# Keeping both halves of split projection weights in DRAM, instead of the low half alone

## The chip, the cores and the metric

One core of one Trainium2 chip runs the whole program. The metric is the device time of one execution in microseconds (us). A kernel's time is the median of its runs; beside it stands one execution that the profiler recorded, and all durations below come from that one. The engines are PE (TensorE, with PEld for its weight loads), DVE (VectorE), ACT (ScalarE), POOL (GpSimd) and SP (SyncE, which here only issues transfers).

## The reference, cut to what matters

The program is one decoder block on 1024 tokens of width 1024. What matters here are its three dense projections, which run for every token:

```
h    = rms_norm(x, norm1_g) * (1 + scale1) + shift1
proj = h @ w_in + b_in                  # 1024 x 2304: q, k, v and three conv inputs
mix  = concat([attn, conv]) @ w_out + b_out          # 1024 x 1024
x    = x + gate1 * mix
h2   = rms_norm(x, norm2_g) * (1 + scale2) + shift2
q    = h2 @ w_query                     # 1024 x 2048: 16 half-queries of 128
# top-16 of 128 keys per half-query, top-16 pairs, then 128 experts per token:
x    = x + gate2 * sum_k gate_k * gelu(h2 . peer_u[idx_k]) * peer_v[idx_k]
y    = rms_norm(x, final_g)
```

All arrays are float32.

## The kernel before

**Two parts.** The *front* computes everything up to the choice of experts, for three groups of token tiles one after the other: `GROUPS = [[0,1,2],[3,4,5],[6,7]]`, a tile being 128 tokens. They are called g0, g1 and g2. The *dense part* (from line 1073) then multiplies five tiles with all 16384 experts (A at line 1133, V at line 1179), while three tiles are done by gathering rows (lines 960 to 990). The dense part's order is written out by hand (`manual_schedule`, line 1323). In the front, the order on each engine is made by the scheduler from its own timeline; the program's order is only what it starts from.

**A projection block.** The weights lie in DRAM as 42 blocks of 1024 x 128 (18 of `w_in`, 8 of `w_out`, 16 of `w_query`), each 512 KB. A group passes through all 42, so 126 blocks are used in all. To keep float32 precision, a weight block is split into a high part H (rounded to the type fp32r) and a low part L = w - H; the activations are split likewise. `lin` (line 269) does three products for each of two halves q of the block, in this order: H x hH, H x hL, L x hH, four matmuls each, so 24 matmuls for a block. L is first used at the ninth matmul of a block (and at the ninth of its second half's twelve), H at the first.

**Where H and L come from.** `Weights.load` (line 215) runs one block ahead of `lin` in the program's order. In all three groups it loads the raw block (line 223, tag `wraw`, two buffers) and lets ACT cast each half to H (line 230, tag `wH`, four buffers, that is two blocks). In g0, POOL computes L (line 232), and one block later SP writes L to a DRAM tile `low` (line 225). In g1 and g2, L is read back from `low` (line 235) into its buffers (tag `wL`, four). A buffer of H or of L can be refilled when the matmuls of the block two before have read it; a raw buffer as soon as its block's two casts are done (in g0 also the two subtractions). All of these transfers are issued by SP, in order, together with the loads of x (line 352), of the adaptive-norm weights (`wada`, line 750, in g0 only), of the keys (line 631) and the stores of `x1` (line 610) and `h2` (line 623).

**What runs beside it.** In g0, DVE works through `wada` (lines 754 and 756) in the first 130 us. In g1 and g2, `dense_gates1` (line 817) builds the gate matrices of the dense tiles: DVE, POOL and ACT make one-hot rows `oh` (lines 834, 843, 847), PE multiplies them (G, line 857), ACT copies the result to `stg` (line 858) and stores it to DRAM (`G_d`, line 860, 2 MB a store, 20 stores, issued from ACT's queue). In the query stage of each group (16 blocks), ACT copies the projection out (line 640), PE multiplies it with the keys (`pk`, line 643), and DVE takes the top 16 (lines 141 to 145). ACT further evicts the output projection (`os`, line 585) and normalises rows (line 321).

Of the kernel before, what the change touches and what calls it, by code (L numbers as in the profile page):

```python
# [9 lines left out]
F32 = mybir.dt.float32  # L10
F32R = mybir.dt.float32r
# [7 lines left out]
P = 128  # L19
# [3 lines left out]
NC = D // P  # L23
# [61 lines left out]
def block_kernel(  # L85
# [18 lines left out]
    nc = tc.nc  # L104
    cst = ctx.enter_context(tc.tile_pool(name="cst", bufs=1))
    dr = ctx.enter_context(tc.tile_pool(name="dr", bufs=1, space=bass.MemoryType.DRAM))
# [46 lines left out]
    with ExitStack() as fctx:  # L153
        sl_ = slx.enter_context(tc.tile_pool(name="sl", bufs=1, side="right"))
        fs = fctx.enter_context(tc.tile_pool(name="fs", bufs=1))
# [46 lines left out]
        class Weights:  # L202


            def __init__(self):
                self.src = [(w_in, k) for k in range(18)] + [(w_out, k) for k in range(NC)]
                self.src += [(w_query, k) for k in range(16)]
                self.n = len(self.src)
                self.src *= len(GROUPS)
                self.at, self.ready = 0, []  # L210

                self.low = [dr.tile([P, 2, NC // 2, P], F32, name=f"low{k}") for k in range(self.n)]
                self.keep = []

            def load(self):
                if self.at == len(self.src):
                    return
                dram, k = self.src[self.at]
                name = f"{self.at}"
                low, first = self.low[self.at % self.n], self.at < self.n  # L220
                self.at += 1
                raw = fs.tile([P, NC, P], F32, tag="wraw", name=f"raw_{name}", bufs=2)
                nc.sync.dma_start(raw.rearrange("p c j -> p (c j)"), dram[k])
                while self.keep:
                    nc.sync.dma_start(*self.keep.pop(0))
                for q in range(2):
                    src = raw[:, q * (NC // 2) : (q + 1) * (NC // 2), :]
                    H = fs.tile([P, NC // 2, P], F32R, tag="wH", name=f"H_{name}_{q}", bufs=4)
                    L = fs.tile([P, NC // 2, P], F32R, tag="wL", name=f"L_{name}_{q}", bufs=4)
                    nc.scalar.copy(H, src)  # L230
                    if first:
                        nc.gpsimd.tensor_tensor(L, src, H.bitcast(F32), op=ALU.subtract)
                        self.keep.append((low[:, q], L.bitcast(F32)))
                    else:
                        nc.sync.dma_start(L.bitcast(F32), low[:, q])
                    self.ready.append((H, L))

            def take(self):
# [11 lines left out]
        class Front:  # L250
# [18 lines left out]
            def lin(self, name):  # L269
# [3 lines left out]
                for o, w, a, n in self.chunks:  # L273
                    ps = bank("a", f"lin_{self.key}{name}_{a}")
                    k = 0
                    for q, (H, L) in enumerate(parts):
                        for wt, h in ((H, self.hH), (H, self.hL), (L, self.hH)):
                            for c in range(NC // 2):
# [601 lines left out]
        def finish(i, acc):  # L880


            def load(name, src):
                t = row(f"{name}{i}")
                nc.sync.dma_start(t, src)
                return t

            g2 = load("g2", g2_d[0].partition_broadcast(P))
            yield
            yield  # L890
            yield
            nc.vector.tensor_tensor(acc, acc, g2, op=ALU.mult)
            xr = load("xr", x1_d[i])
            yield
            yield
            yield
            nc.vector.tensor_tensor(acc, acc, xr, op=ALU.add)
            fg = load("fg", final_g.partition_broadcast(P))
            yield
            ss = cst.tile([P, 1], F32, tag="ssf", name=f"ssf{i}", bufs=2)  # L900
            nc.scalar.activation(xr, acc, AF.Square, accum_out=ss)
            nc.scalar.activation(ss, ss, AF.Sqrt, scale=1.0 / D, bias=eps)
            yield
            yield
            r = cst.tile([P, 1], F32, tag="rf", name=f"rf{i}", bufs=2)
            nc.vector.reciprocal(r, ss)
            nc.vector.scalar_tensor_tensor(xr, acc, r, fg, op0=ALU.mult, op1=ALU.mult)
            yield
            nc.sync.dma_start(out[i * P : (i + 1) * P, :], xr)
# [163 lines left out]
    def dense_experts():  # L1073
# [19 lines left out]
        def split_U(b, part):  # L1093
            if part == 0:
                H = dp.tile([P, NC, P], F32R, tag="UH", name=f"UH{b}", bufs=2)
                nc.scalar.copy(H, Ur[b])  # L1096
# [312 lines left out]
```

## Time and profile before

| | us |
|---|---|
| median of three runs | 2824.21 |
| lowest and highest run | 2823.27, 2829.01 |
| the profiled execution, its own time | 2822.61 |
| its span, first to last instruction | 2820.8 |
| g0 in the trace | 0 to about 318 |
| g1 | about 318 to 667 |
| g2 | about 667 to 980 |
| dense part | about 980 to 2821 |

A stage is named by its group and its weights: g0-in, g1-o, g2-q and so on. The limits are read from the first and last matmuls of each group's blocks. The projections, with all that the change touches, end with g2; nothing in the dense part reads a projection weight.

### The profile page before, as it was taken

To read this page: it belongs to the slowest core of one execution; us is meant where nothing else is said; L and a number is where in the kernel's file an instruction comes from. 1 tells how busy PE (TensorE), PEld (TensorE's weight loads), DVE (VectorE), ACT (ScalarE), POOL (GpSimd) and SP (SyncE) were. 2 spreads that over 40 slices of the span, in tenths; PEclk is the share of its full clock that TensorE was granted. 3 is DMA by queue.
4 is the path that set the end of the run, shared out by engine and by line. 5 is a ranking of instruction groups with operands and counts; after the bars stand their busy time and mean duration, and the time that the engine had idled before them with its cause. 6 is when DMAs were issued, how large, how long until landed. Compare 5 with 4: busy or idle time off the path is not lost.

```text
span 2820.8 us, 44152 instructions
## 1 busy us (share of the span) xinstructions
PE 2642.3 (94%) x15358; PEld 2405.9 (85%) x15358; DVE 2165.8 (77%) x4645; ACT 1033.5 (37%) x2219; POOL 1696.2 (60%) x1726
## 2 busy tenths in 40 slices
PE   5998989988898869999999999999999999999997
PEld 4788977888788869999999899999998899999996
DVE  8835996879786877787777777777877777777776
ACT  3345555664667432222222222222222322222222
POOL 2334533523333247778777677777776777777771
PEclk9999999999999989999999999999999999999999
DMA  9757669986689949898889898989888888889884
GB/s 345 285 182 245 210 201 290 277 290 210 171 224 263 293 132 342 311 339 327 327 321 332 286 350 315 341 310 338 321 325 324 331 325 327 326 324 334 313 326 145
DMA packets 418268, 816.70 MB, mean 290 GB/s; under 512 B 192630, under 2 KB 198774, under 8 KB 418044
## 3 DMA queue, kind: packets, MB, share of 16 engines
q0 software_dynamic: 110592, 402.70, 38.8%
q1 hardware_dynamic: 143292, 369.24, 37.2%
q10 hardware_dynamic: 164160, 41.94, 6.9%
q8 instruction: 120, 1.97, 0.3%
q14 instruction: 104, 0.85, 0.1%
HBM read 739.83 MB, written 73.94 MB: 288 GB/s over the span
## 4 chain that ended last, share of the span: by engine, by line
PE 72%; DVE 13%; DMA 5%; issue 4%; ACT 3%; POOL 2%; SPq 0%; ACTq 0%; DVEq 0%; POOLq 0%
PE A L1133 29%; PE V L1179 29%; PE G L857 3%; PE lin_g1in L279 2%; DVE oh L834 2%; DVE adaacc L756 2%; DMA G_d<-stg 1%; PE lin_g0o L279 1%; DMA wada<-in_w_ada_dram 1%; PE lin_g2in L279 1%; PE po L430 1%; DVE Skg L143 1%; DVE ti L145 1%; PE lin_g2o L279 1%; DVE ti L142 1%
## 5 line engine op out<-in xcount | busy, mean ns | idle before, releaser
L960 POOL DMA_INDIRECT u<-in_peer_u_dram,idx x384 | 365.8, 952 | 264.5 <-DVE u L981 126.7
L1179 PE MATMUL V<-VH,WH 128*128 128x512 f32 x1280 | 501.4, 392 | 12.9 <-DVE acc_d L1186 10.3
L988 DVE SCALAR_TENSOR_TENSOR acc<-v,wv,acc 128x1024 f32<-128x1024 f32 x381 | 489.4, 1285 | 15.1 <-DMA v<-in_peer_v_dram,idx 10.9
L1179 PE MATMUL V<-VL,WH 128*128 128x512 f32 x1280 | 500.1, 391 | 0.0
L1179 PE MATMUL V<-VH,WL 128*128 128x512 f32 x1280 | 499.3, 390 | 0.0
L960 POOL DMA_INDIRECT v<-in_peer_v_dram,idx x384 | 363.5, 947 | 210.7 <-DVE u L981 69.1
L981 DVE SCALAR_TENSOR_TENSOR u<-u,h 128x1024 f32<-128x1024 f32 x384 | 457.7, 1214 | 5.8 <-DMA u<-in_peer_u_dram,idx 5.8
L1138 ACT ACTIVATE A<-A 128x384 f32<-128x384 f32 (+1 forms) x256 | 107.7, 422 | 955.7 <-PE A L1133 940.9
L1133 PE MATMUL A<-hDH,UH 128*128 128x384 f32 (+1 forms) x2048 | 345.5, 311 | 18.7 <-ACT UH L1096 18.1
L1116 POOL TENSOR_TENSOR VL<-V,VH 128x512 fp32r<-128x512 f32 x256 | 332.0, 1310 | 34.9 <-ACT VH L1112 32.6
L1133 PE MATMUL A<-hDH,UL 128*128 128x384 f32 (+1 forms) x2048 | 343.3, 310 | 8.5 <-POOL UL L1100 8.5
L1133 PEld LDWEIGHTS A<-hDH,UH 128*128 128x128 f32 x2048 | 321.9, 190 | 29.5 <-ACT UH L1096 18.9
L1133 PE MATMUL A<-hDL,UH 128*128 128x384 f32 (+1 forms) x2048 | 342.9, 310 | 0.0
L1100 POOL TENSOR_TENSOR UL<-U,UH 128x1024 fp32r<-128x1024 f32 x128 | 308.8, 2413 | 31.9 <-ACT UH L1096 29.7
L1133 PEld LDWEIGHTS A<-hDH,UL 128*128 128x128 f32 x2048 | 311.8, 189 | 9.8 <-POOL UL L1100 9.8
L1150 DVE TENSOR_TENSOR A<-A,Gb 128x384 f32<-128x384 f32 (+1 forms) x256 | 126.2, 498 | 248.3 <-ACT A L1138 243.6
L1133 PEld LDWEIGHTS A<-hDL,UH 128*128 128x128 f32 x2048 | 312.6, 190 | 0.0
L1179 PEld LDWEIGHTS V<-VH,WH 128*128 128x128 f32 x1280 | 241.3, 188 | 60.7 <-DVE acc_d L1186 12.0
L847 POOL TENSOR_TENSOR oh<-oh,gT 128x512 f32<-128x512 f32 x120 | 131.3, 1095 | 261.8 <-DVE oh L834 207.5
L1179 PEld LDWEIGHTS V<-VH,WL 128*128 128x128 f32 x1280 | 241.3, 188 | 51.4
L1179 PEld LDWEIGHTS V<-VL,WH 128*128 128x128 f32 x1280 | 241.3, 189 | 45.3
L1186 DVE TENSOR_TENSOR acc_d<-acc_d,V 128x512 f32<-128x512 f32 x310 | 211.7, 683 | 84.9 <-PE V L1179 84.8
(313 smaller groups left out, 4190.8 us busy)
## 6 DMA issues: line engine op xcount, KB each, us to landing
U<-in_peer_uT_dram SPq DMA_DIRECT2D x128, 512.0 KB, 7.7
V<-in_peer_v_dram SPq DMA_DIRECT2D x256, 256.0 KB, 3.8
L<-low SPq DMA_DIRECT2D x168, 256.0 KB, 4.0
G_d<-stg ACTq DMA_DIRECT2D x20, 2048.0 KB, 16.7
Gb<-G_d SPq DMA_DIRECT2D x64, 640.0 KB, 7.4
raw<-in_w_in_dram SPq DMA_DIRECT2D x54, 512.0 KB, 4.7
wada<-in_w_ada_dram SPq DMA_DIRECT2D x48, 512.0 KB, 6.8
raw<-in_w_query_dram SPq DMA_DIRECT2D x48, 512.0 KB, 5.2
```

The source lines that it names most:

```text
L279: nc.tensor.matmul(ps[:, :w], wt[:, c, :], h[:, q * (NC // 2) + c, o : o + w], start=(k == 0), stop=(k == 3 * NC - 1),)
L847: nc.gpsimd.tensor_tensor(og, og, gT[:, t0 : t0 + 4].unsqueeze(2).to_broadcast([P, 4, NK]), op=ALU.mult)
L960: nc.gpsimd.indirect_dma_start(out=t, out_offset=None, in_=peer_u if which == "u" else peer_v, in_offset=bass.IndirectOffsetOnAxis(ap=idx[ ...
L981: nc.vector.scalar_tensor_tensor(t, t, 1.0, h2[i], op0=ALU.mult, op1=ALU.mult, accum_out=av[i][:, j : j + 1])
L988: nc.vector.scalar_tensor_tensor(acc[i], t, wv[i][:, j : j + 1], acc[i], op0=ALU.mult, op1=ALU.add)
L1100: nc.gpsimd.tensor_tensor(L, Ur.pop(b), Up[b][0].bitcast(F32), op=ALU.subtract)
L1116: nc.gpsimd.tensor_tensor(L, Vr.pop(v), Vp[v][0].bitcast(F32), op=ALU.subtract)
L1133: nc.tensor.matmul(ps[:, : n * P], u[:, c, :], h[:, c, sl], start=(k == 0), stop=(k == 3 * NC - 1))
L1138: nc.scalar.activation(w, w, AF.Gelu)
L1150: nc.vector.tensor_tensor(w3, w3, g, op=ALU.mult)
L1179: nc.tensor.matmul(ps, w[:, ts_], v, start=(n == 0), stop=(n == 3 * CB - 1))
L1186: nc.vector.tensor_tensor(accs[0][:, t, hs], accs[0][:, t, hs], ps, op=ALU.add)
```

## The change

The first group writes both H and L of each half to DRAM, in one tile `HL`, and the second and third groups read that tile back. In those two groups there is no raw load and no cast any more.

```diff
-                self.low = [dr.tile([P, 2, NC // 2, P], F32, name=f"low{k}") for k in range(self.n)]
+                self.kept = [dr.tile([P, 2, 2, NC // 2, P], F32, name=f"kept{k}") for k in range(self.n)]
...
                 name = f"{self.at}"
-                low, first = self.low[self.at % self.n], self.at < self.n
+                kept, first = self.kept[self.at % self.n], self.at < self.n
                 self.at += 1
-                raw = fs.tile([P, NC, P], F32, tag="wraw", name=f"raw_{name}", bufs=2)
-                nc.sync.dma_start(raw.rearrange("p c j -> p (c j)"), dram[k])
+                if first:
+                    raw = fs.tile([P, NC, P], F32, tag="wraw", name=f"raw_{name}", bufs=2)
+                    nc.sync.dma_start(raw.rearrange("p c j -> p (c j)"), dram[k])
                 while self.keep:
                     nc.sync.dma_start(*self.keep.pop(0))
                 for q in range(2):
-                    src = raw[:, q * (NC // 2) : (q + 1) * (NC // 2), :]
-                    H = fs.tile([P, NC // 2, P], F32R, tag="wH", name=f"H_{name}_{q}", bufs=4)
-                    L = fs.tile([P, NC // 2, P], F32R, tag="wL", name=f"L_{name}_{q}", bufs=4)
-                    nc.scalar.copy(H, src)
+                    HL = fs.tile([P, 2, NC // 2, P], F32R, tag="wHL", name=f"HL_{name}_{q}", bufs=4)
+                    H, L = HL[:, 0], HL[:, 1]
                     if first:
+                        src = raw[:, q * (NC // 2) : (q + 1) * (NC // 2), :]
+                        nc.scalar.copy(H, src)
                         nc.gpsimd.tensor_tensor(L, src, H.bitcast(F32), op=ALU.subtract)
-                        self.keep.append((low[:, q], L.bitcast(F32)))
+                        self.keep.append((kept[:, q], HL.bitcast(F32)))
                     else:
-                        nc.sync.dma_start(L.bitcast(F32), low[:, q])
+                        nc.sync.dma_start(HL.bitcast(F32), kept[:, q])
                     self.ready.append((H, L))
```

A write in g0 grows from 256 to 512 KB (84 of them). In g1 and g2 a block is read by two transfers of 512 KB, where it was one of 512 KB (raw) and two of 256 KB (L); the bytes are the same. H and L of a half now share one buffer.

## Rows read from the trace of the kernel before

**Rows 1.** The profile's page: span, engines' busy time, lines of the chain that ended last.

```profile
span 2820.8 us, 44152 instructions
...
PE 2642.3 (94%) x15358; PEld 2405.9 (85%) x15358; DVE 2165.8 (77%) x4645; ACT 1033.5 (37%) x2219; POOL 1696.2 (60%) x1726
...
PE A L1133 29%; PE V L1179 29%; PE G L857 3%; PE lin_g1in L279 2%; DVE oh L834 2%; DVE adaacc L756 2%; DMA G_d<-stg 1%; PE lin_g0o L279 1%; DMA wada<-in_w_ada_dram 1%; PE lin_g2in L279 1%; PE po L430 1%; DVE Skg L143 1%; DVE ti L145 1%; PE lin_g2o L279 1%; DVE ti L142 1%
```

**Rows 2.** Busy time by stage; last columns: PE clock, DMA share, GB/s.

```profile
46.00:130.00 84.00, 81.13 (x435) 69.28 (x435) 76.23 (x140) 34.54 (x83) 31.84 (x22) 0.98 0.85 306
...
222.00:318.00 96.00, 86.69 (x515) 84.46 (x513) 73.19 (x453) 53.66 (x115) 57.07 (x123) 0.95 0.72 242
...
497.00:568.00 71.00, 65.69 (x448) 62.87 (x448) 57.75 (x76) 47.81 (x130) 37.76 (x37) 0.98 0.91 273
...
896.00:980.00 84.00, 74.06 (x578) 72.68 (x577) 69.09 (x347) 42.13 (x97) 24.61 (x76) 0.92 0.90 282
980.00:2820.00 1840.00, 1787.09 (x9997) 1630.03 (x9995) 1414.21 (x2153) 508.77 (x991) 1330.43 (x1129) 0.99 0.86 312
```

**Rows 3.** Groups of ACT in 318 to 980: count, busy us, mean ns, idle before.

```profile
L230 ACT CAST H<-raw 128x512 fp32r<-128x512 f32 x165 | 99.6, 619 | 107.9 <-PE lin_g1in L279 31.6 <-PE lin_g1q L279 23.5 <-PE lin_g2in L279 19.9
```

**Rows 4.** Waits of PE in 318 to 667: us in total, times, longest.

```profile
PE pkg L643 <- ACT qqsg L640: 5.0, 3, 3.0
PE oTg L590 <- ACT osg L585: 3.1, 4, 1.8
```

**Rows 5.** Waits of PE in 667 to 980, same columns.

```profile
PE lin_g2q L279 <- DMA L<-low: 6.8, 3, 5.7
PE oTg L590 <- ACT osg L585: 3.9, 2, 2.7
...
PE pkg L643 <- DMA keyg<-in_keysT_dram: 3.1, 1, 3.1
...
PE lin_g2o L279 <- ACT H L230: 2.4, 1, 2.4
```

**Rows 6.** Two pieces of the chain that ended last: start, us, what.

```profile
336.77 15.01 PE lin_g1in L279 x85
...
764.56 3.83 PE lin_g2in L279 x32
```

**Rows 7.** DMA issues in 46 to 130: count, KB each, median us to landing.

```profile
low<-L SPq DMA_DIRECT2D x21, 256.0 KB, 6.1
raw<-in_w_in_dram SPq DMA_DIRECT2D x10, 512.0 KB, 7.4
```

**Rows 8.** DMA issues in 230 to 318, same columns.

```profile
low<-L SPq DMA_DIRECT2D x28, 256.0 KB, 3.1
raw<-in_w_query_dram SPq DMA_DIRECT2D x12, 512.0 KB, 3.9
```

**Rows 9.** DMA issues in 318 to 980, same columns.

```profile
L<-low SPq DMA_DIRECT2D x165, 256.0 KB, 4.1
G_d<-stg ACTq DMA_DIRECT2D x20, 2048.0 KB, 16.7
...
raw<-in_w_query_dram SPq DMA_DIRECT2D x32, 512.0 KB, 5.5
```

**Rows 10.** Line 235 in 497 to 568: time from issue to landing.

```profile
DMA to landing us min/median/max: 4.1/9.1/10.9
```

**Rows 11.** Line 235 in 896 to 976: time from issue to landing.

```profile
DMA to landing us min/median/max: 2.8/5.2/6.6
```

**Rows 12.** Timeline of ACT's queue, 950 to 970: one store of G_d.

```profile
953.08 0.37 ACTq L860 DMA_DIRECT2D G_d<-stg  x1
```

**Rows 13.** Timeline of SP's queue, 950 to 970: issues after that store.

```profile
953.59 0.33 SPq L235 DMA_DIRECT2D L<-low  x1
...
959.66 0.44 SPq L631 DMA_DIRECT2D keyg<-in_keysT_dram  x1
968.42 0.33 SPq L223 DMA_DIRECT2D raw<-in_w_query_dram  x1
```

## The prediction

> **What bounds the kernel now.** I read the page first, to see where the time lies [rows 1]. PE is busy 94% of the 2820.8 us, and the chain that ended last is led by A and V of the dense part. The stage table shows why the dense part is out of reach of this change: it takes the last 1840 us, PE is busy 1787 of them, and it reads no projection weight [rows 2]. So the question is only when the front ends, now at about 980 us. A time saved or lost before that moves the end by as much, if it lies on the chain there.
>
> Inside the front the bound changes from stage to stage [rows 2]. In 46 to 130 (g0-in) PE is busy 81 of 84 us and DVE 76, while the DMA engines are busy 85%. In 497 to 568 (g1-o) PE is busy 66 of 71 us with the DMA at 91%; in 896 to 980 (g2-q) it is 74 of 84 us with the DMA at 90%. ACT, whose work is removed, is busy 47.8 of 71 us and 42.1 of 84 us in the last two. It is no bound by its sum. It can only matter by its order: an eviction that PE waits for may stand behind a cast.
>
> The waits of PE are the second view. In g1 and g2 its waits for ACT that a cast could lengthen are qqs 5.0 us and os 3.1 us [rows 4], os 3.9 us and the cast itself 2.4 us [rows 5]: 14.4 us. Its waits for transfers of SP's queue are 6.8 us for L and 3.1 us for the keys, all in g2-q [rows 5].
>
> **The change part by part.**
>
> *Casts removed in g1 and g2.* 84 blocks of two casts are 168; 165 of them lie in 318 to 980, with 99.6 us of busy time and 107.9 us in which ACT stood before a cast [rows 3]. That standing is mostly for PE to give back the H buffer, and everything behind it on ACT stands too. But most of this is idle time of an engine that is not the bound. From below the gain is 0 (the casts wait at places where nothing else was ready), from above all 14.4 us of those four waits. The evictions themselves stay, and they need their own time: PE waits for an os or qqs copy even when ACT is free. I take a third: -5 us.
>
> *Writes doubled in g0.* 84 writes grow by 256 KB, 22 MB in all. In 46 to 130, 21 writes add 5.5 MB. The stage moves 306 GB/s at a share of 0.85, so 360 GB/s when full: 15.3 us of transfer time, where 0.15 x 84 = 12.6 us are free [rows 2]. The writes stand in SP's order ahead of the next raw load and of `wada`, for which DVE waits. Bounds: 0 (all in the gaps) and +15 us; the excess over the gaps is 2.7 us, and the gaps are not where the writes are, so I take +4.
>
> In 222 to 318 (g0-q) the rate when full is 242 / 0.72 = 336 GB/s [rows 2], so each raw load behind a grown write comes 0.78 us later. A raw buffer serves every second block, so a block loses 0.39 us at most; over the 24 blocks of g0-o and g0-q that is 9 us, and 0 where PE is behind anyway. PE is busy 86.7 of 96 us in g0-q [rows 2], so most is hidden: +2. Sum for g0: +6, bounds 0 and +24.
>
> The H cast of g0 now also waits for the write-out of the block two before. In g0-q a write lands 3.1 us after its issue [rows 8], plus 0.78 us, against two blocks' time of some 10 us (a block is at least 24 matmuls, 4.24 us, see below): hidden, 0. In g0-in 6.1 us [rows 7] plus some 0.7 us stand against two blocks of 8.4 us (84 us for ten raw loads [rows 7]): hidden too. Without that cover ACT's whole queue would stand, evictions included; that case is inside the upper bound.
>
> *The read in g1 and g2.* The bytes are the same. What changes is when they may move. Raw had two buffers of its own, so it came ahead of the H buffer; a load of HL can start only when PE has left the half block of two blocks before. And HL is needed at a block's first matmul, L was needed at the ninth.
>
> A matmul of g1's blocks takes 15.01 / 85 = 0.177 us, one of g2's 3.83 / 32 = 0.120 us [rows 6], so a block is 4.24 us or 2.87 us of pure matmuls. If blocks run back to back, the first half of HL has one and a half blocks to land: 6.4 us in g1, 4.3 us in g2. Half an L had eight matmuls more: 7.8 and 5.3 us. A transfer of 256 KB lands in 4.1 us, one of 512 KB in 5.5 us (medians of L and of raw query weights [rows 9]). So the slack falls from 3.7 to 0.9 us in g1 and from 1.2 to -1.2 us in g2.
>
> Blocks are rarely back to back. In g2-q, 16 blocks take 84 us, 5.25 us each; there the first half has 2 x 5.25 - 1.43 = 9.1 us on average, against a median of 5.2 us and a longest of 6.6 us for L today [rows 11]. Only tight pairs stall. I count five of 16, each by 1.2 us: +6. Bounds: 0, and 16 x 1.2 = 19 us.
>
> In g1-o, G_d stores make L land in 9.1 us, up to 10.9 us [rows 10]. Eight blocks take 71 us, so 8.9 us each, and the first half has 2 x 8.9 - 2.1 = 15.7 us on average. Blocks are uneven there; I count two that lose the eight matmuls, 1.4 us each, and one more in g1-q: +4. Bounds 0 and 8 x 1.4 = +11. The short run of blocks in g2-in stalls a little as well, but the long DVE-led stretch behind it takes that up: 0.
>
> *Fewer transfers on SP's queue.* After the G_d store issued at 953.08 SP issued seven transfers (the rows of 953.59 to 959.66; one row that is left out holds three), then stood from 960.1 until 968.42, about when the store landed [rows 12, 13]: the eighth transfer waited for it. A block of g2-q is four issues now (raw, two of L, keys) and three afterwards. Seven issues then last 2.33 blocks instead of 1.75, so SP comes to stand 0.58 x 5.25 = 3 us later. The waits for L and keys are 9.9 us [rows 5]; bounds -9.9 and 0, I take -3.
>
> **The sum.** -5 + 6 + 6 + 4 - 3 = +8 us. On the profiled execution, 2822.6 us (1.8 us more than its span), that is 2830.6. The median of the runs lies 1.6 us above that execution; the forecast is 2831.
>
> The Trainium skill, page "DMA: Bandwidth & Descriptors", section "Anatomy of one DMA — SWDGE (gpsimd) path", gives a fit, for GpSimd's own path, of about 2.0 us plus the bytes over 436 GB/s. By it 512 KB would land in an estimated 3.2 us, the read in g1 and g2 would cost nothing, and the sum would be -2. The 5.5 us of [rows 9] speak against it for loads in company.
>
> **The rivals.**
>
> *Faster: ACT's order pays.* Place: the gate pipeline and the evictions of g1 and g2, which stand behind casts that wait for PE. For it: 107.9 us of standing on ACT [rows 3]. Against it: PE's four waits are 14.4 us in all. If two thirds of them go (-10), SP's standing after the stores shrinks (-6), and the reads stay hidden as their averages say (0), then with +5 in g0 it is -11: 2812. It decides if HL lands before the first matmul in nearly all blocks.
>
> *No change: everything is hidden.* The loads have 9.1 us on average in g2-q, PE hides g0's writes but for some +3, and ACT gives -3. Then it is 2823 to 2825. The fit named above leads here. Against it: the DMA is at 85 to 91% in three of the stages shown, so a later start is seldom free.
>
> *Much slower: the lost lead.* The raw buffers held two blocks in advance; without them every G_d store (16.7 us to land [rows 9]) is met with only two blocks on hand. If each block of g2-q stalls (+19), g1-o likewise (+11) and g0 costs +6, with -5 of ACT, it is +31: 2854. Against it: the averages of 9.1 and 15.7 us.
>
> That the change does not do what it says is hardly possible: loads and casts are taken out of the program. But the scheduler orders the front anew, and may move G or the evictions by some us either way; this is in the width.
>
> **How the numbers follow.** 0.2% of the time is 5.6 us, about what a measurement of this kernel can tell from no change. Chances: the forecast (+2 to +16) 0.45, of which 0.09 within 0.2%; no change 0.23; faster 0.23, of which 0.02 within 0.2%; much slower 0.09. So faster by over 0.2% is 0.21, within it 0.34, slower 0.45. The range takes in most of the forecast's bounds and part of both sides: 2812 to 2847. The forecast's own range is 2826 to 2840.
>
> **What the profile would show.** If I am right: ACT's busy time some 104 us lower; g0's last block ends 3 to 9 us later, with raw loads landing later in 46 to 130; PE waits for HL appear at first matmuls of g2-q, 10 us or more in all; and the dense part starts at about 988. PE's waits behind os and qqs shrink by 5 us. It would be wrong if HL is hardly ever waited for (then 2824 or less), if g0 does not move, or if the order of the front comes out otherwise, so that PE's waits for DVE or POOL change by more than all of this.

## The result and the profile after

The changed kernel takes 2854.25 us in the median of four runs (2850.38 to 2857.84), the kernel before 2825.39 in four runs beside them (2823.27 to 2829.01). The ratio is 1.0102, 95% interval 1.0081 to 1.0123: some 29 us slower. The prediction was 2831 us, 2812 to 2847, and slower with a chance of 0.45. The sign was the likeliest one; the time lies outside the range.

The page of the changed kernel, against [rows 1]:

```profile
span 2848.6 us, 43793 instructions
...
PE 2647.9 (93%) x15358; PEld 2414.5 (85%) x15358; DVE 2162.3 (76%) x4645; ACT 940.5 (33%) x2051; POOL 1693.2 (59%) x1726
...
HBM read 739.83 MB, written 95.96 MB: 293 GB/s over the span
...
HL<-kept SPq DMA_DIRECT2D x168, 512.0 KB, 5.3
...
kept<-HL SPq DMA_DIRECT2D x84, 512.0 KB, 5.3
```

The change did what it says: ACT has 93 us less to do, 96 MB are written where before had 74, and 168 reads of 512 KB take the place of raw and low. The span is 27.8 us longer all the same.

Busy time by stage of the changed kernel, with the columns of [rows 2]; the last row is the dense part, from its first A:

```profile
46.00:130.00 84.00, 76.60 (x415) 66.37 (x415) 76.69 (x156) 33.47 (x83) 27.50 (x18) 0.96 0.91 350
...
917.40:1012.40 95.00, 75.28 (x587) 73.55 (x585) 72.31 (x376) 29.33 (x73) 25.94 (x81) 0.91 0.86 268
1012.40:2848.60 1836.20, 1785.75 (x9984) 1628.98 (x9984) 1409.66 (x2123) 505.89 (x987) 1326.70 (x1123) 0.99 0.86 312
```

The dense part lasts 1836.2 us; before it lasted 1836.9 (983.9 to the end of the span). So the whole loss is in the front: its end, the first A, has moved from 983.9 to 1012.4, by 28.5 us (these are the times of single matmuls; the 318 and 980 of the sections ahead are rounder). In g2-q, the row above it, PE has 75.3 us of work in 95.0 us; before the stage took 87.5. From first matmul to first matmul the loss is 5.4 us in g0, 6.4 in g1-in, 1.1 in g1-o, 4.5 in g1-q, 2.2 in g2-in, 1.4 in g2-o and 7.5 in g2-q: three quarters of it lie outside the stage that this section looks at next.

The waits of PE in 318 to 1012, against [rows 4, 5]:

```profile
PE G L858 <- POOL oh L848: 23.2, 21, 5.6
PE lin_g2q L280 <- DMA HL<-kept: 16.4, 5, 6.8
...
PE lin_g1q L280 <- DMA HL<-kept: 3.7, 1, 3.7
...
PE pkg L644 <- DMA keyg<-in_keysT_dram: 3.0, 1, 3.0
PE lin_g2in L280 <- DMA HL<-kept: 2.8, 6, 0.9
...
PE pkg L644 <- ACT qqsg L641: 2.6, 3, 1.0
```

With 0.8 us in g1-in PE waits 23.7 us for blocks that are read back, 16.4 of them in five places of g2-q. Where the waits lie is seen in the chain that ended last, in g2-q, of the changed kernel and then of before:

```profile
939.03 19.86 DMA G_d<-stg
...
959.39 4.63 DMA HL<-kept
964.01 0.04 issue
964.06 2.93 PE lin_g2q L280 x12
...
978.84 18.30 DMA G_d<-stg
...
997.62 4.48 DMA HL<-kept
```

```profile
953.08 15.28 DMA G_d<-stg
...
968.85 3.95 DMA L<-low
```

Twice the end of the front hangs on a store of G_d and then on a read of HL; before it hung on one once, and 5.7 of PE's 6.8 us for L lay there [rows 5]. SP's queue after the first of these stores:

```profile
940.04 0.32 SPq L624 DMA_DIRECT2D h2d<-xng  x1
940.45 2.09 SPq L236 DMA_DIRECT2D HL<-kept  x2
942.60 1.12 SPq L632 DMA_DIRECT2D keyg<-in_keysT_dram  x1
943.81 1.04 SPq L624 DMA_DIRECT2D h2d<-xng  x1
944.95 1.75 SPq L236 DMA_DIRECT2D HL<-kept  x2
958.95 0.33 SPq L632 DMA_DIRECT2D keyg<-in_keysT_dram  x1
959.39 0.85 SPq L236 DMA_DIRECT2D HL<-kept  x2
```

As before [rows 13], seven transfers go out and the eighth goes when the store has landed. Here the seven were gone by 946.7, and SP stood 12.2 us. Behind the second store it was seven again, and SP stood 9.1 us. The trace's record of each issue says why it is the eighth: it names the semaphore that the landing raises, and in g2-q the issues of SP and ACT together take eight semaphores in turn, in both kernels. The eighth issue after a store comes round to the store's own semaphore, and first waits for it. The HL issued at 959.39 landed 4.63 us later, and PE waited 6.4 us for it; behind the second store it waited 6.8 us.

To compare kernels I add up, for the front, PE's idle time (gaps of over 150 ns) by what ended it. All in us; "blocks" are weights that a transfer brings, "first lin" and "first A" are the ends of the front, "busy" is PE between them. Each row is one profiled execution; its front can lie some 10 us from what the timed runs give, so times are taken from the ratios, and this table only says where.

```
                 first lin  blocks keys  ACT   POOL  DVE   busy   first A
before             46.5      7.5   3.1  46.9  25.3   7.6  845.8    983.9
before, again      46.7      7.7   3.5  45.9  25.3   7.7  851.2    989.3
after              49.6     23.7   3.0  45.0  30.6   8.3  851.5   1012.4
e1 ring of six     46.0      0.3  11.2  52.8  26.3   9.3  859.4   1005.5
e2 write alone     49.7     10.7   0    51.3  28.8   8.8  860.6   1011.0
s1 shared tile     46.8      8.7   0    47.0  26.7   7.5  858.3    995.3
s2 separate        51.7     14.4   3.2  47.5  25.1   7.7  849.4    999.9
s3 other rates     46.6     13.4   0    38.5  26.6   6.9  854.5    987.3
h1 write, sep.     49.8      8.6   3.2  46.0  26.5  10.5  845.7    991.2
h2 read, sep.      46.7     17.7   0.9  40.4  33.3   7.6  852.5   1000.1
h3 read, ring      44.4      0    16.1  48.5  30.5   3.3  842.4    986.0
h4 all, ring       45.3      0    21.0  79.4  28.5   3.8  859.4   1038.5
k1 no casts        47.2     17.8   4.3  37.5  29.8   6.9  854.2    999.0
k2 read, lead      46.2      0    22.2  37.0  29.8   6.0  855.1    997.2
k3 two not kept    46.1     15.4   5.5  46.0  29.6  14.7  859.5   1018.5
k4 all three       46.0      3.6  15.3  53.9  28.3   9.8  854.8   1012.5
m1 before, fixed   45.1      0     0   177.4  33.8  67.0  927.6   1252.0
m2 after, fixed    45.1      6.6   7.0 143.1  37.5  73.9  917.7   1231.8
```

For the change the rows "before" and "after" give: first lin +3.1, blocks +16.2, ACT -1.9, POOL +5.3, DVE +0.7, busy +5.7. That is 29.1 for the 28.5 us; keys are the same. The busy term is no more than what lies between two profiles of the kernel before (845.8 and 851.2). The sum tells what PE waited for, not what each wait cost: in s3 below, the waits for blocks are 5.9 us longer than before and those for ACT 8.4 us shorter, at no loss of time.

### The profile page after: what moved, and what is told of

Its sections match the earlier page's. It is cut to its first block, busy times and chain, and to the rows that moved or that the text cites. A ratio compares the mean times of both kernels' runs of the same rounds, so it can differ in the third digit from the quotient of the medians.

```text
span 2848.6 us, 43793 instructions
## 1 busy us (share of the span) xinstructions
PE 2647.9 (93%) x15358; PEld 2414.5 (85%) x15358; DVE 2162.3 (76%) x4645; ACT 940.5 (33%) x2051; POOL 1693.2 (59%) x1726
## 4 chain that ended last, share of the span: by engine, by line
PE 75%; DMA 9%; DVE 8%; issue 3%; ACT 2%; POOL 2%; SPq 0%; ACTq 0%; DVEq 0%; POOLq 0%
PE A L1134 30%; PE V L1180 29%; PE G L858 3%; DMA G_d<-stg 3%; PE lin_g1in L280 2%; DVE oh L835 2%; PE lin_g0in L280 1%; PE lin_g0o L280 1%; DMA HL<-kept 1%; DMA wada<-in_w_ada_dram 1%; PE lin_g2in L280 1%; PE lin_g1q L280 1%; PE po L431 1%; PE lin_g2q L280 1%; PE lin_g2o L280 1%
```

## The experiments

Three theories stood at first. *Lost lead*: reads start too late, for want of raw blocks fetched ahead. *Writes*: the first group's added 22 MB. *Order*: the compiler orders the front's instructions anew from its own forecast, and the new order is worse. Ratios are to the kernel before, timed on the same chip beside each run; 0.001 is 2.8 us.

**One part at a time.** e1: the change, raw and HL in one ring of six buffers.

```diff
-raw = fs.tile([P, NC, P], F32, tag="wraw", name=f"raw_{name}", bufs=2)
+raw = fs.tile([P, 2, NC // 2, P], F32R, tag="wHL", name=f"raw_{name}", bufs=6).bitcast(F32).rearrange("p a c j -> p (a c) j")
...
-HL = fs.tile([P, 2, NC // 2, P], F32R, tag="wHL", name=f"HL_{name}_{q}", bufs=4)
+HL = fs.tile([P, 2, NC // 2, P], F32R, tag="wHL", name=f"HL_{name}_{q}", bufs=6)
```

> The changed kernel, but raw and HL tiles share one ring of six 4 KB buffers, so the room that raw leaves idle in the second and third group holds a third block of HL. Theory 'lost lead' (HL can be fetched only two blocks ahead, where raw had two more buffers): 15 to 23 us come back, 2831 to 2839. Theory 'writes' (the first group's doubled writes and what they delay are the loss): nothing comes back, 2850 to 2858. Theory 'order' (the front's instructions simply came out in a worse order): no relation to the lead, anywhere in 2840 to 2865.

2848.71 us, ratio 1.0071 (1.0049 to 1.0092). The waits for blocks are gone (0.3 us), and most of the loss stays: keys cost 11.2 us now.

e2: the first group writes HL, the others fetch raw, cast, and read the low half, as before.

```diff
-self.keep.append((low[:, q], L.bitcast(F32)))
+self.keep.append((kept[:, q], HL.bitcast(F32)))
-nc.sync.dma_start(L.bitcast(F32), low[:, q])
+nc.sync.dma_start(L.bitcast(F32), kept[:, q, 1])
```

> One part alone: the first group writes H and L (512 KB a half) as in the changed kernel, in the shared HL buffer, but the second and third group load raw, cast H and read back only L as before. Theory 'lost lead': only the first group's price is left, +5 to +9 us against before, 2830 to 2835. Theory 'writes': most of the loss stays, 2845 to 2855. Theory 'order': undecided, 2820 to 2850.

2855.47 us, ratio 1.0087 (1.0063 to 1.0111).

e3: the first group keeps the low parts only; the others read the HL of the first block each time.

```diff
-self.keep.append((kept[:, q], HL.bitcast(F32)))
+if self.at == 1:
+    self.keep.append((kept[:, q], HL.bitcast(F32)))
+self.keep.append((low[:, q], L.bitcast(F32)))
```

> The other part alone: the second and third group read HL (512 KB a half, no raw load, no cast), but the first group writes only L, as before. So that this needs no more writes, H and L of the first block alone are kept and every read takes that block, so later groups multiply with the first block's weights: same bytes, same sizes, other values. Theory 'lost lead': the loss of the second and third group stays, +18 to +24 us against before, 2843 to 2850. Theory 'writes': close to before, 2820 to 2830. Theory 'order': undecided, 2820 to 2855.

2860.25 us, ratio 1.0121 (1.0098 to 1.0145). In its trace PE waits 19.2 us for blocks. So either half alone costs about what the whole costs. Neither "lead" nor "writes" allows that. e2 and e3 share with the change that H and L lie in one tile.

e4: the kernel before with `bufs=1` for raw.

> The kernel before with one raw buffer instead of two, nothing else changed: casts, sizes and writes as before, but half of the lead is gone. Theory 'lost lead': slower than before by 8 to 25 us, 2833 to 2850. Theories 'writes': no change from the second and third group, and only what the first group's subtraction holds up, 2823 to 2832. Theory 'order': undecided.

2968.22 us, ratio 1.0493 (1.0467 to 1.0518). The stall is ACT's, some 24 us of PE's idle time in g2-q alone: the casts wait for raw, and the evictions behind them too. It shows that casts can hold up PE, but it says nothing of a read into HL.

**The tile and the order.** s1: before, with H and L as two parts of one tile.

```diff
-H = fs.tile([P, NC // 2, P], F32R, tag="wH", name=f"H_{name}_{q}", bufs=4)
-L = fs.tile([P, NC // 2, P], F32R, tag="wL", name=f"L_{name}_{q}", bufs=4)
+HL = fs.tile([P, 2, NC // 2, P], F32R, tag="wHL", name=f"HL_{name}_{q}", bufs=4)
+H, L = HL[:, 0], HL[:, 1]
```

> The kernel before with one edit: the high and the low half-block lie in one tile of two parts instead of two tiles; every transfer, cast and subtraction is as before. 'Shared tile' (one tile of both parts is released only when the last reader of either is done, and the two parts are ordered as one thing): 15 to 25 us slower than before. 'Lost lead' and 'writes': within 5 us of before, since nothing is read or written otherwise. 'Order' (any edit of the front makes the program's order anew, and the order of before was a good one): 5 to 25 us slower, with PE's waits in the input and output-key stages longer and not its waits for blocks.

2832.38 us, ratio 1.0033 (1.0020 to 1.0046).

s2: the change, with H and L in tiles of their own, four transfers a block; against the change:

```diff
-self.keep.append((kept[:, q], HL.bitcast(F32)))
+self.keep.append((kept[:, q, 0], H.bitcast(F32)))
+self.keep.append((kept[:, q, 1], L.bitcast(F32)))
...
-nc.sync.dma_start(HL.bitcast(F32), kept[:, q])
+nc.sync.dma_start(H.bitcast(F32), kept[:, q, 0])
+nc.sync.dma_start(L.bitcast(F32), kept[:, q, 1])
```

> The changed kernel with one edit: high and low are kept in DRAM and read back as in the change, but lie in two tiles, so that there are four transfers of 256 KB for each block instead of two of 512 KB. 'Shared tile': 0 to 10 us slower than before, so 19 to 29 faster than the change. 'Lost lead' (the read waits for its tile, with no raw block fetched ahead) and 'writes': 25 to 32 us slower than before, as the change. 'Order': anywhere from 5 to 30 us slower.

2849.14 us, ratio 1.0081 (1.0061 to 1.0100).

s3: other rates for the gates' work; s4: the kernel before, once more.

```diff
-RATE_G = {("p", 1): 0.65, ("q", 1): 0.0, ("p", 2): 1.25, ("q", 2): 0.4}
+RATE_G = {("p", 1): 0.66, ("q", 1): 0.0, ("p", 2): 1.27, ("q", 2): 0.4}
```

> The kernel before with two numbers of the scheduler's table changed by 1.5%: the rates at which the gates' work is strewn among the projections of the output keys and queries' groups, 0.65 to 0.66 and 1.25 to 1.27. No instruction, tile or transfer is added or removed; only the order on the engines is another. 'Order': 5 to 25 us slower. 'Lost lead', 'shared tile' and 'writes': within 3 us of before.

2826.12 us, ratio 1.0004 (0.9991 to 1.0017).

> The kernel before, unchanged, profiled on the chip of these runs, so that the stages of the others have a row of before beside them. Every theory: the first matmul of the dense part at 984 us within 3 us, and a time within 0.3% of before.

2829.72 us in its one run; the first A is at 989.3, later than expected, so much do two profiles of one kernel differ. The shared tile alone costs some 9 us, less than expected; with it taken away the change still costs 23. Another order of the gates' work costs nothing: "order" is not simply that any new order is worse.

**Writes and reads in separate tiles.** h1: the first group writes H too, and nobody reads it.

```diff
+self.keep.append((high[:, q], H.bitcast(F32)))
 self.keep.append((low[:, q], L.bitcast(F32)))
```

> The first group writes the high half-blocks to DRAM as well (two transfers of 256 KB more for each of its 42 blocks), from tiles of their own; nobody reads them, and the second and third group fetch raw, cast and read the low parts as before. 'Writes' (the added 21 MB and what they hold up in the first group are the loss): 12 to 20 us slower than before, all of it ahead of the second group. 'Lost lead' and 'order': 0 to 5 us slower.

2832.88 us, ratio 1.0030 (1.0013 to 1.0048).

h2: the later groups fetch no raw and cast nothing.

```diff
-nc.scalar.copy(H, src)
 if first:
+    nc.scalar.copy(H, raw[:, half, :])
...
 else:
+    nc.sync.dma_start(H.bitcast(F32), low[:, q])
     nc.sync.dma_start(L.bitcast(F32), low[:, q])
```

> The second and third group fetch no raw weights and cast nothing: both half-tiles are read back from DRAM, in tiles of their own, and nothing more is written than before. Both are read from the kept low parts, so this kernel's products of the later groups are not the reference's; bytes, transfers and waits are those of a kernel that had the high parts there. 'Lost lead' (with no raw block fetched ahead, a read waits until the half-block two places earlier is released): 12 to 20 us slower than before, none of it ahead of the second group, and PE's waits for blocks of 15 us and over. 'Writes': 0 to 5 us slower, or faster by the casts that are gone.

2845.23 us, ratio 1.0079 (1.0057 to 1.0100).

h3 is h2, and h4 the change with separate tiles (s2), with one ring for the half-blocks of raw, H and L:

```diff
-H = fs.tile([P, NC // 2, P], F32R, tag="wH", name=f"H_{name}_{q}", bufs=4)
-L = fs.tile([P, NC // 2, P], F32R, tag="wL", name=f"L_{name}_{q}", bufs=4)
+H = fs.tile([P, NC // 2, P], F32R, tag="wHL", name=f"H_{name}_{q}", bufs=12)
+L = fs.tile([P, NC // 2, P], F32R, tag="wHL", name=f"L_{name}_{q}", bufs=12)
```

> As the run before this in the list, but raw, high and low half-blocks share one ring of twelve buffers of 256 KB, so that a read in the later groups may start three blocks ahead instead of two, in the same memory. Both half-tiles are again read from the kept low parts, so the later groups' products are not the reference's. 'Lost lead': PE's waits for blocks under 3 us, and 10 to 15 us faster than the run without the ring, so within 5 us of before on either side. 'Writes': as the run without the ring, within 3 us.

2835.59 us, ratio 1.0044 (1.0028 to 1.0059).

> The whole change (high and low parts kept by the first group and read back), in separate half-tiles, and with the ring of twelve buffers of 256 KB. 'Lost lead': 0 to 8 us slower than before. 'Writes': 12 to 20 us slower. If both count and add up, it lies above the ring with reads alone by as much as the added writes alone lie above before.

2879.07 us, ratio 1.0199 (1.0177 to 1.0222). The writes cost some 8 us and the reads 22, of which the ring gives back 10. But 8 and 22 and the shared tile's 9 are more than 29, and the ring makes the whole change worse: PE's waits for ACT grow to 79.4 us, 42.1 of them in the first group, where each cast takes a buffer of the ring. Of the expectations, 'lost lead' has h2 nearly right and h3's waits; but h1 lies between the two theories, h3 is 13 us from before instead of within 5, and h4 is far above both.

**What is the cost of each?** k1: before, without the later groups' casts; raw is fetched and not read.

```diff
-nc.scalar.copy(H, src)
 if first:
+    nc.scalar.copy(H, src)
...
 else:
     nc.sync.dma_start(L.bitcast(F32), low[:, q])
+    H = L
```

> The kernel before, without the casts of the second and third group: raw is still fetched and nobody reads it, the low part stands in for the high one in those groups (their products are not the reference's). It shows what the casts alone are worth. 'Casts on the path' (ACT's order pays): 8 to 15 us faster than before. 'Casts covered' (the gates' matmuls wait for selections that hang on DVE, so ACT's free time buys nothing): within 4 us of before. 'Order' (removing them makes a worse order): 5 to 12 us slower.

2844.58 us, ratio 1.0067 (1.0046 to 1.0088). This looks like the price of a worse order, but it is no clean test: with no cast to wait for, raw ran ahead. The DMA rows of k1 in 318 to 515 show 49 raw loads, where before had 20:

```profile
raw<-in_w_in_dram SPq DMA_DIRECT2D x25, 512.0 KB
...
raw<-in_w_query_dram SPq DMA_DIRECT2D x16, 512.0 KB
raw<-in_w_out_dram SPq DMA_DIRECT2D x8, 512.0 KB
```

The stages of k1 (g1-o, and g2 as a whole) and, in the second fence, g2 of before, again:

```profile
514.80:597.20 82.40, 69.05 (x431) 65.97 (x431) 56.58 (x80) 44.63 (x123) 36.24 (x36) 0.89 1.02 336
```

```profile
694.60:999.00 304.40, 267.34 (x2016) 247.14 (x2016) 248.84 (x749) 141.27 (x364) 103.84 (x165) 0.96 0.65 174
```

```profile
671.60:989.30 317.70, 273.46 (x2015) 252.50 (x2015) 249.80 (x750) 182.67 (x445) 102.62 (x166) 0.94 0.80 232
```

While raw crowds in, the DMA engines are full in g1-o (share 1.02) and g1's three stages take 373.5 us, where before, again has 341.6 (330.0 to 671.6). In g2, with no raw left, k1 is 13.3 us faster than before. There both the casts and the raw loads are gone, so this does not tell the one from the other; k1 shows only that the same front is slower where transfers are crowded and faster where they leave room.

k2: h2, with every third block of the later groups read into the two raw buffers.

```diff
+if first or self.at % 3:
     H = fs.tile([P, NC // 2, P], F32R, tag="wH", name=f"H_{name}_{q}", bufs=4)
     L = fs.tile([P, NC // 2, P], F32R, tag="wL", name=f"L_{name}_{q}", bufs=4)
+else:
+    W = fs.tile([P, NC, P], F32, tag="wraw", name=f"W_{name}_{q}", bufs=2).bitcast(F32R)
+    H, L = W[:, : NC // 2], W[:, NC // 2 :]
```

> The run with reads alone, in which every third block of the later groups is read into the two raw buffers, which are idle there, so that a read may start three blocks ahead; the first group is untouched. High parts are again read from the kept low parts (the later groups' products are not the reference's). 'Lost lead': PE's waits for blocks under 3 us and 10 to 18 us faster than with two blocks of lead, so 2827 to 2835. 'Order' and 'casts': as without the lead, 2840 to 2850.

2839.02 us, ratio 1.0042 (1.0028 to 1.0055). As forecast no wait for blocks is left, and by the ratios it is some 10 us better than h2. But it is not back at before, since PE now waits 22.2 us for keys, 12.8 of them in g2-q. From its chain there:

```profile
968.59 14.01 DMA G_d<-stg
983.99 3.96 DMA keyg<-in_keysT_dram
```

SP stands behind the store as ever. With more blocks at hand, the first transfer that PE misses behind it is the keys.

k3: the change, the first two blocks not kept.

```diff
+k0 = self.at % self.n
+kept, first, skip = self.kept[k0], self.at < self.n, k0 < 2
...
-if first:
+if first or skip:
...
-self.keep.append((kept[:, q], HL.bitcast(F32)))
+if not skip:
+    self.keep.append((kept[:, q], HL.bitcast(F32)))
```

> The changed kernel, but the first two blocks of the weights are not kept: the later groups fetch them raw and cast them, as before. With that the four writes ahead of the adaLN weights are gone. 'Early writes': the first matmul 3 to 4 us earlier than in the change, and 4 to 8 us faster than it (2846 to 2850). 'Lead' and 'shared tile': within 3 us of the change.

2853.31 us, ratio 1.0090 (1.0069 to 1.0111). The first matmul is back at 46.1, as expected, and the time is not: the 3 us are lost again in the stages behind.

k4: s2, with the edits of k2 and k3.

> The whole change with the three costs that the runs named mended: high and low in separate half-tiles, the first two blocks not kept, and every third block of the later groups read into the idle raw buffers. If the three are the causes: within 8 us of before, on either side. If the added writes between 60 and 318 us cost by themselves: 8 to 14 us slower than before.

2850.61 us, ratio 1.0091 (1.0070 to 1.0113). The three mended together bring nothing over s2. That the three are the causes, to be added up, is refuted. In the table its waits for keys (15.3) and for ACT (53.9) stand where those for blocks stood.

**The same order for both.** m1 and m2: before and after, the order of the front on PE, ACT, POOL and SP fixed to that of the program text.

```diff
+fixed = ExitStack()
+fixed.enter_context(tc.manual_schedule(engines=ORDERED - {mybir.EngineType.DVE}))
 def front(q, hH, hL):
...
+fixed.close()
 chosen = chain(choose(6), choose(7))
```

> The kernel before, with the order of the front on PE, ACT, POOL and SP fixed to that of the program text (DVE's order is still made by the compiler). It is the base for the next run only; no theory says how it stands to the kernel before. 'Order' leads one to expect another time than before's by tens of us, either way.

3092.20 us, ratio 1.0951 (1.0929 to 1.0972).

> The changed kernel with the order of the front fixed in the same way: PE's and POOL's instructions come in exactly the order of the run before this in the list, ACT's in the same without the casts. 'Order': within 8 us of that run, on either side (casts gone, added transfers). 'Transfers' (the reads' lost lead and the writes cost what they cost in any order): 20 to 35 us slower than that run, with PE waiting for the blocks read back and for casts held up by writes.

3074.98 us, ratio 1.0900 (1.0881 to 1.0919). The traces bear out the order: all 5371 records of PE in the front of m1, and all 603 of POOL, come in the same order in m2, where between before and the change only some 4300 of PE's do. In this one order the change is 17 us faster by the medians, 14 by the ratios; neither theory had that. PE's waits in g1 and g2 of m1, and then of m2:

```profile
PE pkg L643 <- ACT qqsg L640: 45.9, 32, 14.4
```

```profile
PE pkg L644 <- ACT qqsg L641: 22.4, 31, 1.5
...
PE pkg L644 <- DMA keyg<-in_keysT_dram: 7.0, 1, 7.0
```

In the order of the program text the casts stand ahead of the copies of qqs that PE needs, and taking them out gives PE 23.5 us there, 34.3 for ACT in all. The transfers cost in this order too: blocks and keys rise from 0 to 13.6 us. In the compiler's order the same wait for qqs falls from 7.9 us over the front (5.0 of it in [rows 4]) to 2.6 us (the rows of the changed kernel above), and all waits for ACT only from 46.9 to 45.0.

## Why the prediction was wrong

*Where the loss would be.* Right: only in the front, the dense part unchanged (its start was forecast at 988 and measured at 1012.4). The sum itself has a small slip: 2830.6 and the 1.6 us between execution and median make 2832.2, not 2831, and the rivals' 2812 and 2854 leave out the 1.6 us too.

*Writes in g0, +6.* The size is about right: the second group starts at 331.9 instead of 326.5, 5.4 us later (330.0 in the other profile of before, so this is not sharp), and in h1 the writes alone cost 8 us of timed runs. A part that the prediction did not have are 3.1 us before the first matmul, where four writes of 512 KB go out among the first `wada` loads, and DVE stands 3.51 us for `wada` at 41.45. The sign that was to show the rest is absent: raw loads in 46 to 130 land in 7.5 us, before in 7.4.

*Read in g1 and g2, +10.* Mis-sized: +16.2. In g2-q the waits rose by 9.6 us (forecast 6), in g1-q by 3.0, in g2-in by 2.8, where I took 0, and in g1-in by 0.8. In g1-o, the place of most of my other +4, there was none. Five stalls in g2-q was the forecast count, but that is luck: two of them, 6.4 and 6.8 us, make most of it. They are not tight pairs of blocks at 1.2 us, they stand behind the two G_d stores of the chain. HL lands there as here:

```profile
DMA to landing us min/median/max: 3.8/6.3/9.2
```

That is 6.3 us where the forecast took 5.5. The fit of the Trainium skill that the prediction weighs (page "DMA: Bandwidth & Descriptors", section "Anatomy of one DMA — SWDGE (gpsimd) path") would have put it at an estimated 3.2 us; the trace does not agree with it for loads in company.

*Casts, -5.* ACT lost 93 us of work, PE's waits for ACT 1.9 us. The four waits that the prediction named were shortened, and by more than it took: from 14.4 to 5.3 us in g1 and g2 (os 7.0 to 2.7, qqs 5.0 to 2.6, the cast 2.4 to none). But other waits for ACT rose in the new order (for the squares of a norm, line 450, from 0.8 to 4.3 in g1-in) and took the gain back. m1 and m2 show that in one fixed order, with casts ahead of what PE needs, the gain is there.

*Fewer issues on SP, -3.* Wrong in sign. SP's waits in g2-q, of before and then of after:

```profile
SPq L223 <- DMA G_d<-stg: 8.3, 1, 8.3
SPq L623 <- DMA G_d<-stg: 7.7, 1, 7.7
```

```profile
SPq L632 <- DMA G_d<-stg: 21.3, 2, 12.2
```

SP stood 21.3 us instead of 16.0. The seven issues did not last longer: behind the two stores of g2-q they took 17.3 us together before and 16.9 after; behind the first one after, several were ready at once, and two stores of h2 were among the seven. And the two G_d stores took longer to land, 18.0 and 15.3 us before, 19.9 and 18.3 after. Why they did is not shown.

*The rest, 0.* The step "may move G or the evictions by some us either way; this is in the width" left out 5.3 us more of waits for POOL, from its one-hot rows, and 5.7 us of PE's busy time, which two profiles of one kernel differ by too.

So the step that failed is the offset of the reads: they were set at +10, by tight pairs of blocks, against -8 of casts and SP's issues, where the trace shows +16.2 against -2.0 (ACT -1.9, keys -0.1). In its place: SP stands longer behind the G_d stores, not shorter, and behind them lie 13.2 us of PE's waits for HL, where 5.7 lay for L. The offset is 12.2 of the 20.5 us between the forecast +8 and the 28.5 of the trace; nearly all else is what was put at 0. These are PE's waits added up; that they are the cause in full is not shown.

*The rivals.* "Much slower: the lost lead" has the measured time, 2854, by luck, and one piece of its mechanism: a G_d store met with too few blocks on hand is on the chain. Its parts were not met: 19 us in g2-q (9.6 measured), 11 in g1-o (none). And lead alone does not undo it (e1, k2): the next transfer behind the store is late then. "Faster: ACT's order pays" holds in the fixed order only.

*What stays open.* Why the parts don't add up: shared tile 9, writes 8, reads 22, whole 29, and with one tile either half about as much. Each edit changes the compiler's order on every engine as well as the transfers, and no run separates the two at the order of before; m1 and m2 do so in an order with more room. That the stand of SP behind the stores is the root in g2-q is read from the chains of four kernels (before, the change, h3, k2); a kernel with these stores out of SP's way, say with a semaphore of their own, was not tried. No version here beats the kernel before.

## What to carry to other kernels

Work taken off an engine is worth what the waits for that engine are worth in the order that runs now, not its busy time: 93 us of casts were worth 1.9 here, and 34 where the order put them in the way. A load that needs its consumer's buffer loses the lead that a staging buffer gave it. Extra buffers gave back some 10 of 22 us here and passed the rest of the wait to the next load of the same queue: ask what stands first in the queue when it is held up, and what holds it up. And where a compiler orders the program, add no prices from single edits; test at a fixed order, and in the real one.

## What the runs showed of the hardware

After each of the four G_d stores of g2-q, two before and two after, SP issued seven transfers and then stood until the store had landed: 7.7 and 8.3 us before, 12.2 and 9.1 us after. In the records the eighth issue waits for the very semaphore that the store raises, one of eight that are taken in turn. So these rows show the program's bookkeeping, and no limit of the queue.

A stage with gaps can cost PE's own work too. The first stage of m1, with the columns of [rows 2]:

```profile
45.10:272.00 226.90, 162.55 (x673) 130.58 (x673) 94.15 (x197) 53.44 (x127) 50.41 (x38) 0.76 0.54 179
```

PE idles 64 of 227 us there, 41.9 of them in waits for DVE's adaptive norm; its granted clock averages 0.76 of 2.4 GHz, so it was at the lower of its two levels for a good part of the stage, and the matmuls keep it busy 162.6 us, where the same stage of before has 129.4 of 133.4 us at a mean of 0.97. Of the 268 us by which m1's front is longer than before's, 82 are PE's busy time. Two such stages make no rule.
